# Dealing the copies of K and V anew over GpSimd, VectorE and ScalarE in a tree-masked attention kernel

## The chip, the cores and the metric

The kernel runs on one core of a Trainium2 chip. The metric is the device time of one execution in microseconds (us). The engines of the core are called by the profile's names: PE (TensorE: matmul, with PEld for its weight loads), DVE (VectorE), ACT (ScalarE), POOL (GpSimd), SP (SyncE). Loads and stores are DMA transfers; here nearly all of them are issued by GpSimd.

## The reference

Attention over 8 x 12 = 96 heads, 512 positions, 64 channels, with a mask that lets each position see itself and its ancestors in a binary tree (the parent of i is (i - 1) // 2):

```python
scale = 1.0 / np.sqrt(dim)
mask = np.zeros((seq, seq))
for i in range(seq):
    mask[i, i] = 1
    parent = i
    while parent > 0:
        parent = (parent - 1) // 2
        mask[i, parent] = 1
scores = np.einsum('bhqd,bhkd->bhqk', Q, K) * scale
scores = scores + (1 - mask) * (-1e9)
weights = np.exp(scores - np.max(scores, axis=-1, keepdims=True))
weights = weights / (np.sum(weights, axis=-1, keepdims=True) + 1e-10)
return np.einsum('bhqk,bhkd->bhqd', weights, V).astype(np.float32)
```

Q, K, V and the result are fp32 in HBM, 12.58 MB each.

## The kernel before

**Tiling.** The 96 heads are taken as 48 pairs i = 0 to 47; four pairs (8 heads) are a group g = i // 4, and 16 heads (two groups) are one block o of V. Because a node sees only its ancestors, most of the 512 x 512 scores are never computed: the nodes are reordered into units of 32, and each pair needs one full score tile (`scores1`, lines 494 and 499, exponentials at line 510) and a second, sparser one (`scores2`, lines 519 and 525, exponentials at line 541). The mask comes from small code matrices that are multiplied in (lines 494 and 519).

**The steps of a pair.** `transpose(i)` turns K and Q of a group on PE into the PSUM tile `kqp`, of which there is one (lines 375 and 397; four calls for a group: the first two turn K, the last two Q); `evac(i)` copies it to the SBUF tile `kq` on VectorE (line 444 after the first and the second call, line 436, one large copy, after the fourth). `scores1` and `scores2` multiply into the PSUM tiles `s1` and `s2`, one of each, and ScalarE takes the exponentials. `values(i)` multiplies with V into the PSUM tile `ob`, of which there is one (line 552), and `norm(i)` divides on VectorE (reciprocal at line 585, multiplication at line 590) into the output tile. `store(g)` sends a finished group of 8 heads, 1 MB, from GpSimd (line 598); the last four pairs are sent singly (line 607).

**Copies.** Two kinds of copy lie beside this. `lay_beside` (line 324) lays the two halves of K or of Q of one group side by side in `Kbeside` or `Qbeside` (two buffers each) before they can be transposed; it is needed for groups 3 to 11. `spread` (line 306) copies one of ten parts of a V block, for eight heads, from the loaded tile `vst` to the operand tile `vt` (two blocks): parts 0 to 3 are 32 x 512 words, parts 4 and 5 are 64 x 512, parts 6 to 9 are 32 x 256. All ten parts of eight heads must be there before `values` of the first pair that uses them.

**Order.** All order is written by hand. The engines run their lists in order and wait on semaphores. A start-up string (`EARLY`) holds the first steps; then turn i, for i from 6, runs the tokens "S T V": S is `scores1` and `scores2` of pair i, T is the next `transpose` with its `evac`, V is `values` and `norm` of pair i - 1. In the turns, T runs four pairs ahead of S; `TURNS` may change a turn's tokens: a second T in turn 17 puts T five pairs ahead from there on. L in a turn is a `lay_beside` of K on VectorE. After a turn's tokens come the V copies that `BY_VECTOR` and `BY_SCALAR` give to VectorE and ScalarE in that turn; from block 3 on, `STEADY_VECTOR` and `STEADY_SCALAR` deal parts 0, 1 and 3 to VectorE and part 2 to ScalarE in a fixed rhythm.

**GpSimd's list.** The string `POOL` is GpSimd's whole program: kN, qN, vN load eight heads from head N on (K and Q at line 267, V at line 257; three buffers of K, of Q and of V blocks), KN and QN are `lay_beside` of a group, c and t are V copies (t: parts 6 to 9, and from block 1 on also 4 and 5), x and e prepare the codes and the transposing matrices, sN stores a group, pN a single pair. A load needs a free buffer, so a load of K or Q of group g comes behind the copy of group g - 3.

Of the kernel before, what the change touches and what calls it, by code (L numbers as in the profile page):

```python
# [121 lines left out]
def kernel(  # L122
# [7 lines left out]
    nc = tc.nc  # L130
    B, H, S, D = Q.shape
# [87 lines left out]
    NV = 2  # L219
# [62 lines left out]
    def load_v(h0, n):  # L282
        return load(vsts, vloads, "vst", VB, Vr, h0, n)

    def spread(copy, o, part, h0, h1):

        vt, vst = vts[o % NV][:, :, :, :], vsts[o][:, :, :, :]
# [18 lines left out]
        return copy(out=dst, in_=src)  # L306
# [3 lines left out]
    def lay_beside(copy, name, g):  # L310

        kept = (ksts if name == "K" else qsts)[g]
        to = besides[name, g] = beside.tile([P, GP, 4, 2, D], bf16, name=f"{name}beside")
# [10 lines left out]
        copy(out=dst, in_=src)  # L324
# [218 lines left out]
    def values(i):  # L543

        if i < NP - 1:
            obs[i] = ob = psO.tile([P, 2, 512], fp32, name="ob")
        else:
            obs[i] = ob = psS.tile([P, 2, 512], fp32, name="s1")
        e1, e2, vt = ets[i], e2s[i % NE], vts[(2 * i // VB) % NV]

        def product(e, a, t, tile_v, lo=0, hi=128, **flags):
            nc.tensor.matmul(  # L552
                out=ob[lo:hi, a, 65 * t:65 * t + 65],
                lhsT=e[:, a, PLACE[t], lo:hi],
                rhs=vt[:, head(i, a) % VB, tile_v, 0:D + 1],
                **flags,
            )

        def halves(a):
            for t in (0, 1):  # L560
                product(e2, a, t, 1 + SELF[t], 0, 64, start=False, stop=t == 1)
                product(e2, a, t, 1 + t, 64, 128, start=False, stop=t == 1)

        for a in range(2):
            for t in range(4):
                product(e1, a, t, 0, start=t == 0, stop=False)
            for t in (2, 3):
                product(e2, a, t, 1 + t, start=False, stop=False)
            if i == NP - 1:
# [34 lines left out]
    def store_pair(eng, i, a=0, n=2):  # L604
# [12 lines left out]
    )  # L617

    def pool_program():

        ops = []
        for word in POOL.split():
# [6 lines left out]
            elif kind == "c":  # L629
                o, part, h0, h1 = n  # L630
                ops.append((spread, nc.gpsimd.tensor_copy, o, part, h0, h1))
            elif kind == "t":
                o, h0 = n
                ops += [
                    (spread, nc.gpsimd.tensor_copy, o, part, h0, h0 + KB)
                    for part in (6, 7, 8, 9) + ((), (4, 5))[min(o, 1)]
                ]
            elif kind == "s":
                ops.append((store, nc.gpsimd, n[0]))
# [8 lines left out]
    def ready(op, i):  # L648
# [18 lines left out]
    BY_VECTOR = {  # L667
# [11 lines left out]
    }  # L679
    BY_SCALAR = {  # L680
        0: [(0, 5, 0, 8)],
        4: [(0, 1, 8, 16), (0, 2, 8, 16)],
        7: [(1, 3, 0, 8)],
        8: [(1, 2, 0, 8)],
        11: [(1, 3, 8, 16)],
        12: [(1, 2, 8, 16)],
        13: [(2, 3, 0, 8)],
        15: [(2, 1, 0, 8)],
        17: [(2, 3, 8, 16)],
        18: [(2, 1, 8, 16)],  # L690
    }

    STEADY_VECTOR = {0: 0, 1: 1, 3: 3}
    STEADY_SCALAR = {2: 2}

    def spread_by(copy, table, steady, i):

        todo = list(table.get(i, []))
        for lead, h0 in ((4, 0), (0, 8)):
            o, j = divmod(i + lead, 8)  # L700
            if o >= 3 and o < NH // VB and j in steady:
                todo.append((o, steady[j], h0, h0 + 8))
        for args in todo:
            spread(copy, *args)

    program = pool_program()

# [16 lines left out]
        kept[0] = loads.tile([P, KB, 4, D], bf16, name=name)  # L724
        nc.vector.tensor_copy(out=kept[0][:, 0:2, :, :], in_=first[src][:, :, :, :])
    EARLY = "X K S Q D0 S A0 X6 T X D1 S X T V S T V T V T T A4 S D3 T V S T V"
    TURNS = {11: 'S T L4 V', 17: 'S T V T'}
    done, scored, valued = 1, 0, 0
    pool(-1)
    transpose(0)  # L730
    evac(0)

    def step(token):

        nonlocal done, scored, valued
        kind, n = token[0], token[1:]
# [15 lines left out]
        if kind == "X":  # L752
            spin("s1" if valued else "ob", int(n or 2))
        if kind == "D":
            for args in BY_VECTOR.get(int(n), []):
                spread(nc.vector.tensor_copy, *args)
        if kind == "A":
            for args in BY_SCALAR.get(int(n), []):
# [8 lines left out]
    for i in range(scored, NP + 1):  # L767
        turn = "S T V" if i not in TURNS else TURNS[i]
        for token in turn.split():
            step(token)  # L770
        spread_by(nc.vector.tensor_copy, BY_VECTOR, STEADY_VECTOR, i)
        spread_by(nc.scalar.copy, BY_SCALAR, STEADY_SCALAR, i)
        pool(valued)
        if i == NP - 1:
            store_pair(nc.sync, NP - 2)
# [33 lines left out]
```

## Time and profile before

| | us |
|---|---|
| Median of three runs (lowest to highest) | 133.6 (132.94 to 135.47) |
| The profiled execution, its own time | 132.84 |
| Its span in the profile, first to last instruction | 130.8 |

The span and the execution's own time differ by 2.0 us that lie around the profiled instructions. In the span PE is busy 88%, ACT 76%, POOL 74% and DVE 73%; the granted clock is 0.986. No engine is busy throughout, so the page has to be read by stages and by the chain of waits, and the transfers by their own rows: `DMA share` in a table of stretches is the time that packets took, summed over the 16 DMA engines and divided by 16 times the stretch (packets overlap, so it can be over 1), and GB/s counts what was written: a load reads 4 bytes of HBM for each 2 that it writes, since it converts fp32 to bf16 on the way. "To landing" is the time from the issue of a transfer to its completion.

### The profile page before, as it was taken

What the parts mean: (1) busy time and instruction counts of PE and PEld (TensorE: products, weight loads), DVE (VectorE), ACT (ScalarE), POOL (GpSimd) and SP (SyncE); (2) the same over time, 40 slices, a digit from 0 to 9 for tenths busy, and PEclk for the clock granted to TensorE, in tenths of its full rate; (3) what the DMA queues carried; (4) which work ended last, traced back from release to release, by engine and by line L of the source; (5) the groups of instructions that cost most, each with busy time, mean ns of one, the idle gap of its engine ahead of it and who ended that gap; (6) DMA issues with size and microseconds to landing.
All of it is one profiled execution on the core that took longest, in us unless ns stands there. A gap on an engine that the chain in (4) does not pass through costs nothing.

```text
span 130.8 us, 4949 instructions
## 1 busy us (share of the span) xinstructions
PE 115.4 (88%) x2132; PEld 82.6 (63%) x2133; DVE 95.9 (73%) x179; ACT 99.0 (76%) x160; POOL 96.3 (74%) x149
## 2 busy tenths in 40 slices
PE   4989996999998998995999997989989999989930
PEld 1444565776866676774776875767767777856620
DVE  4236778758958959774989798798998898775460
ACT  4339553787988988886778886887897897899920
POOL 6979978239899999999999999999996930202300
PEclk9999999999999999999999999999999999999995
DMA  4999999999999999999999999999999999999992
GB/s 124 195 185 205 209 185 211 201 211 205 210 197 217 201 206 202 209 205 207 212 199 211 202 209 207 205 210 232 336 220 357 406 401 401 401 402 401 384 352 94
DMA packets 24533, 32.13 MB, mean 246 GB/s; under 512 B 944, under 2 KB 15920, under 8 KB 24512
## 3 DMA queue, kind: packets, MB, share of 16 engines
q0 software_dynamic: 23232, 30.67, 110.9%
q1 hardware_dynamic: 720, 0.70, 1.7%
q10 hardware_dynamic: 560, 0.46, 1.0%
q8 instruction: 16, 0.26, 0.7%
q14 instruction: 5, 0.04, 0.1%
HBM read 37.86 MB, written 12.58 MB: 385 GB/s over the span
## 4 chain that ended last, share of the span: by engine, by line
PE 59%; DVE 25%; POOL 6%; issue 3%; ACT 3%; ACTq 0%; POOLq 0%
PE ob L552 16%; DVE kq L436 7%; PE s L494 7%; DVE of L590 7%; PE kqp L375 7%; PE s L499 6%; PE kqp L397 6%; PE s L519 5%; DVE vt L306 5%; PE s L525 5%; PE s L718 3%; POOL vt L306 3%; PE ob L718 2%; PE kqp L350 2%; DVE rec L585 2%
## 5 line engine op out<-in xcount | busy, mean ns | idle before, releaser
L510 ACT ACTIVATE e<-s 128x1024 bf16<-128x1024 f32 x48 | 49.1, 1023 | 21.3 <-PE s L499 20.9
L306 POOL COPY vt<-vst 32x256 uint32<-32x256 uint32 (+2 forms) x70 | 34.9, 499 | 8.9 <-DMA vst<-in_V_dram 5.7
L541 ACT ACTIVATE e<-s 128x384 bf16<-128x384 f32 (+1 forms) x92 | 41.4, 505 | 0.0
L552 PE MATMUL ob<-vt,e 128*128 128x65 bf16 (+1 forms) x940 | 36.9, 197 | 2.4 <-DVE of L590 2.1
L552 PEld LDWEIGHTS <-e 128*128 128x128 bf16 (+1 forms) x960 | 31.2, 102 | 7.9 <-DVE of L590 3.7
L590 DVE TENSOR_TENSOR of<-ob,rec 128x512 f32<-128x512 f32 x44 | 30.4, 691 | 1.5
L306 DVE COPY vt<-vst 32x512 uint32<-32x512 uint32 (+1 forms) x33 | 20.6, 625 | 1.0
L499 PE MATMUL s<-kq 64*128 64x512 bf16 x96 | 18.4, 379 | 2.1 <-DVE kq L436 2.1
L525 PEld LDWEIGHTS <-kq 64*128 64x128 bf16 x384 | 16.3, 110 | 6.3
L598 POOL DMA_DIRECT2D out_dram<-of x11 | 9.8, 897 | 13.5 <-DVE of L590 13.5
L585 DVE RECIPROCAL rec<-ob 128x8 f32<-128x8 f32 x47 | 9.6, 204 | 12.8 <-PE ob L552 12.5
L444 DVE COPY kq<-kqp 128x1024 bf16<-128x1024 bf16 x22 | 15.1, 687 | 4.9 <-PE kqp L375 4.4
L525 PE MATMUL s<-kq 64*128 64x160 bf16 (+1 forms) x384 | 17.9, 210 | 0.0
L494 PE MATMUL s<-qcoarse,codes 40*128 40x512 bf16 x88 | 17.2, 387 | 0.0
L519 PE MATMUL s<-qcoarse,codes 40*128 40x480 bf16 x88 | 16.3, 364 | 0.3
L436 DVE COPY kq<-kqp 128x2048 bf16<-128x2048 bf16 x11 | 13.5, 1224 | 2.2 <-PE kqp L397 1.8
L375 PE MATMUL kqp<-mixed,Kbeside 128*128 128x128 bf16 x144 | 11.1, 220 | 2.8 <-POOL Kbeside L324 1.7
L519 PEld LDWEIGHTS <-codes 40*128 40x128 bf16 x96 | 7.6, 95 | 8.4 <-issue 2.0
L306 ACT COPY vt<-vst 32x512 uint32<-32x512 uint32 (+1 forms) x17 | 10.7, 627 | 1.7 <-DMA vst<-in_V_dram 1.3
L397 PE MATMUL kqp<-ptile,Qbeside 128*128 128x128 bf16 x144 | 11.2, 220 | 0.2 <-DVE kq L444 0.2
L375 PEld LDWEIGHTS <-Kbeside 128*128 128x128 bf16 x144 | 8.3, 98 | 4.2 <-POOL Kbeside L324 2.0
L257 POOL DMA_DIRECT2D vst<-in_V_dram x12 | 10.9, 910 | 0.0
(45 smaller groups left out, 102.2 us busy)
## 6 DMA issues: line engine op xcount, KB each, us to landing
out_dram<-of POOLq DMA_DIRECT2D x11, 1024.0 KB, 15.6
vst<-in_V_dram POOLq DMA_DIRECT2D x12, 512.0 KB, 14.0
kst<-in_K_dram POOLq DMA_DIRECT2D x11, 512.0 KB, 11.9
qst<-in_Q_dram POOLq DMA_DIRECT2D x11, 512.0 KB, 12.3
out_dram<-ol POOLq DMA_DIRECT2D x2, 256.0 KB, 5.3
qst<-in_Q_dram POOLq DMA_DIRECT2D x3, 128.0 KB, 7.1
ol<-in_K_dram SPq DMA_DIRECT2D x1, 256.0 KB, 2.9
ol<-in_Q_dram ACTq DMA_DIRECT2D x1, 256.0 KB, 3.2
```

Of the source, the lines that this page charges most:

```text
L306: return copy(out=dst, in_=src)
L375: nc.tensor.transpose(out=dst, in_=src, identity=perm)
L397: nc.tensor.transpose(out=dst, in_=src, identity=eye[:, 0:128])
L436: return nc.vector.tensor_copy(out=dst, in_=src) if x == 3 else None
L494: nc.tensor.matmul(out=columns(g, sp[:, a, :], 0, 512), lhsT=k1code[64 * a:64 * a + CODE_ROWS, :], rhs=query_codes(i, a, 0, 0, 512), start ...
L499: nc.tensor.matmul(out=columns(g, sp[:, a, :], 0, 512), lhsT=keys(i, a, TOP), rhs=queries(i, a, 0, 512), start=False, stop=True,)
L510: nc.scalar.activation(out=dst, in_=src, func=AF.Exp, scale=scale)
L519: nc.tensor.matmul(out=columns(g, flat[:, a, :], 32, 512), lhsT=k2code[64 * a:64 * a + CODE_ROWS, :], rhs=query_codes(i, a, 1, 32, 512), s ...
L525: nc.tensor.matmul(out=columns(g, flat[:, a, :], lo, hi), lhsT=keys(i, a, TILE2[t]), rhs=queries(i, a, lo, hi), start=False, stop=t == 1,)
L541: nc.scalar.activation(out=dst, in_=src, func=AF.Exp, scale=scale)
L552: nc.tensor.matmul(out=ob[lo:hi, a, 65 * t:65 * t + 65], lhsT=e[:, a, PLACE[t], lo:hi], rhs=vt[:, head(i, a) % VB, tile_v, 0:D + 1], **flags,)
L590: nc.vector.tensor_tensor(out=dst, in0=o4[:, a:a + n, :, 0:D], in1=rec[:, a:a + n, :, :].to_broadcast([P, n, 4, D]), op=ALU.mult,)
```

## The change

GpSimd's list `POOL` is another one. It has the same loads and stores, the same copies of Q and the same V copies (parts 4 to 9 from block 1 on; the letter t is split into u for parts 6 to 9 and w for parts 4 and 5). Its order differs: among others v8 and the code preparation come earlier, the load k80 comes before k72, stores s0 and s1 come before the loads v88, k88 and q88, and s2 before q88. Of the K copies it keeps groups 6, 8 and 9; VectorE takes groups 3, 5, 7, 10 and 11 beside group 4, through L tokens in `TURNS`.

The V copies outside GpSimd are 50 as before, but VectorE has 26 instead of 33 and ScalarE 24 instead of 17, and all of them stand in the two tables: the steady rhythm is gone. The tokens D and A, which place a turn's VectorE and ScalarE copies, may now stand anywhere in a turn; without them they come last as before. The second T moves from turn 17 to turn 19.

```diff
     POOL = (
-        "k2.2 q2.2 v0 k4.4 q4.2 q6.2 k8 q8 e v8 c0.6.0.8 c0.7.0.8 c0.8.0.8 c0.9.0.8 x0 x64 k16 q16 v16 k24 q24 v24 "
-        "k32 t0.8 c0.3.8.16 c0.0.8.16 t1.0 K3 v32 q32 Q3 k40 t1.8 v40 q40 v48 t2.0 "
-        "Q4 k48 q48 v56 K5 t2.8 Q5 k56 q56 v64 t3.0 K6 k64 q64 v72 Q6 t3.8 "
-        "k72 q72 K7 Q7 v80 k80 q80 t4.0 K8 v88 s0 Q8 k88 q88 t4.8 s1 K9 Q9 t5.0 s2 K10 s3 Q10 t5.8 s4 K11 Q11 s5 s6 s7 s8 s9 s10 p44 p45 "
+        "k2.2 q2.2 v0 k4.4 q4.2 x0 q6.2 k8 v8 c0.7.0.8 x64 c0.9.0.8 c0.8.0.8 q8 c0.6.0.8 k16 q16 e v16 c0.3.8.16 "
+        "c0.0.8.16 k24 q24 v24 u0.8 k32 v32 u1.0 q32 k40 Q3 v40 w1.0 q40 u1.8 v48 w1.8 w2.0 q48 Q4 k48 u2.0 v56 "
+        "u2.8 w2.8 Q5 k56 q56 k64 Q6 w3.0 K6 q64 u3.0 v64 v72 u3.8 k80 q72 Q7 Q8 k72 q80 w4.0 K8 v80 w3.8 s0 s1 "
+        "K9 Q9 v88 w4.8 u4.0 u4.8 k88 s2 q88 w5.0 Q10 s3 w5.8 s4 s5 Q11 u5.0 s6 u5.8 s7 s8 s9 s10 p44 p45 "
     )
...
     BY_VECTOR = {
         0: [(0, 0, 0, 8), (0, 2, 0, 8), (0, 3, 0, 8)],
         1: [(0, 1, 0, 8), (0, 4, 0, 8)],
-        3: [(0, 4, 8, 16), (0, 5, 8, 16)],
-        7: [(1, 1, 0, 8)],
-        8: [(1, 0, 0, 8)],
-        11: [(1, 1, 8, 16)],
-        12: [(1, 0, 8, 16)],
-        14: [(2, 2, 0, 8)],
-        15: [(2, 0, 0, 8)],
-        17: [(2, 2, 8, 16)],
-        19: [(2, 0, 8, 16)],
+        3: [(0, 4, 8, 16), (0, 5, 8, 16), (0, 2, 8, 16), (0, 1, 8, 16)],
+        6: [(1, 0, 0, 8)],
+        7: [(1, 3, 0, 8)],
+        12: [(2, 2, 0, 8)],
+        13: [(1, 1, 8, 16)],
+        14: [(2, 0, 0, 8)],
+        16: [(2, 0, 8, 16)],
+        17: [(3, 0, 0, 8)],
+        22: [(3, 3, 0, 8)],
+        23: [(3, 3, 8, 16)],
+        24: [(3, 2, 8, 16)],
+        27: [(4, 0, 0, 8)],
+        29: [(4, 0, 8, 16), (4, 1, 8, 16)],
+        33: [(5, 2, 0, 8)],
+        37: [(5, 0, 8, 16)],
+        43: [(5, 3, 8, 16), (5, 2, 8, 16)],
     }
     BY_SCALAR = {
         0: [(0, 5, 0, 8)],
-        4: [(0, 1, 8, 16), (0, 2, 8, 16)],
-        7: [(1, 3, 0, 8)],
-        8: [(1, 2, 0, 8)],
-        11: [(1, 3, 8, 16)],
-        12: [(1, 2, 8, 16)],
-        13: [(2, 3, 0, 8)],
-        15: [(2, 1, 0, 8)],
-        17: [(2, 3, 8, 16)],
-        18: [(2, 1, 8, 16)],
+        7: [(1, 1, 0, 8), (1, 2, 0, 8)],
+        10: [(1, 0, 8, 16), (1, 2, 8, 16)],
+        12: [(1, 3, 8, 16)],
+        14: [(2, 1, 0, 8)],
+        15: [(2, 3, 8, 16)],
+        16: [(2, 3, 0, 8)],
+        17: [(3, 2, 0, 8)],
+        18: [(2, 1, 8, 16), (2, 2, 8, 16)],
+        19: [(3, 1, 0, 8)],
+        23: [(3, 1, 8, 16)],
+        25: [(3, 0, 8, 16)],
+        26: [(4, 2, 0, 8)],
+        29: [(4, 3, 0, 8)],
+        31: [(4, 1, 0, 8), (4, 2, 8, 16)],
+        33: [(5, 0, 0, 8)],
+        36: [(4, 3, 8, 16)],
+        39: [(5, 1, 0, 8)],
+        40: [(5, 3, 0, 8)],
+        41: [(5, 1, 8, 16)],
     }
-    STEADY_VECTOR = {0: 0, 1: 1, 3: 3}
-    STEADY_SCALAR = {2: 2}
...
-    TURNS = {11: 'S T L4 V', 17: 'S T V T'}
+    TURNS = {7: "S T L3 V", 10: "S T L4 V", 12: "S D T V", 13: "S D T V", 14: "S T A L5 V", 17: "S T D V", 19: "S T V T", 21: "S T V L7", 29: "S T D V", 31: "S T A V", 33: "S D T L10 V", 37: "S T D V", 38: "S L11 T V", 40: "S A T V"}
...
     for i in range(scored, NP + 1):
         turn = "S T V" if i not in TURNS else TURNS[i]
         for token in turn.split():
-            step(token)
-        spread_by(nc.vector.tensor_copy, BY_VECTOR, STEADY_VECTOR, i)
-        spread_by(nc.scalar.copy, BY_SCALAR, STEADY_SCALAR, i)
+            step(token, i)
+        if "D" not in turn:
+            step("D", i)
+        if "A" not in turn:
+            step("A", i)
         pool(valued)
```

An entry (o, part, h0, h1) is one V copy: block, part, first and last head of the block. The rest of the diff adds assertions that run while the program is built and hands the turn's number to `step`.

More of the change, by code (lines that the diff above doesn't have):

```diff
@@ L283, in load_v @@
         return load(vsts, vloads, "vst", VB, Vr, h0, n)
+    spreads = set()
+    done = scored = valued = 0
     def spread(copy, o, part, h0, h1):
+        assert 2 * valued >= VB * (o + 1 - NV)
+        spreads.update((o, part, h) for h in range(h0, h1))
         vt, vst = vts[o % NV][:, :, :, :], vsts[o][:, :, :, :]
@@ L312, in lay_beside @@
         kept = (ksts if name == "K" else qsts)[g]
+        assert done >= GP * (g - 1)
         to = besides[name, g] = beside.tile([P, GP, 4, 2, D], bf16, name=f"{name}beside")
@@ L548, in values @@
             obs[i] = ob = psS.tile([P, 2, 512], fp32, name="s1")
+        assert all((2 * i // VB, part, head(i, a) % VB) in spreads for part in range(10) for a in range(2))
         e1, e2, vt = ets[i], e2s[i % NE], vts[(2 * i // VB) % NV]
@@ L631, in pool_program @@
                 ops.append((spread, nc.gpsimd.tensor_copy, o, part, h0, h1))
-            elif kind == "t":
+            elif kind in "uw":
                 o, h0 = n
@@ L635, in pool_program @@
                     (spread, nc.gpsimd.tensor_copy, o, part, h0, h0 + KB)
-                    for part in (6, 7, 8, 9) + ((), (4, 5))[min(o, 1)]
+                    for part in {"u": (6, 7, 8, 9), "w": (4, 5)}[kind]
                 ]
@@ L681 @@
         0: [(0, 5, 0, 8)],
-        4: [(0, 1, 8, 16), (0, 2, 8, 16)],
-        7: [(1, 3, 0, 8)],
-        8: [(1, 2, 0, 8)],
-        11: [(1, 3, 8, 16)],
-        12: [(1, 2, 8, 16)],
-        13: [(2, 3, 0, 8)],
-        15: [(2, 1, 0, 8)],
-        17: [(2, 3, 8, 16)],
-        18: [(2, 1, 8, 16)],
-    }
-    STEADY_VECTOR = {0: 0, 1: 1, 3: 3}
-    STEADY_SCALAR = {2: 2}
[L696 to L704, printed above, removed]
+        7: [(1, 1, 0, 8), (1, 2, 0, 8)],
[17 more added lines that the diff above has]
+        41: [(5, 1, 8, 16)],
+    }
     program = pool_program()
@@ L731, with step @@
     evac(0)
-    def step(token):
+    def step(token, i=0):
         nonlocal done, scored, valued
@@ L754, in step @@
         if kind == "D":
-            for args in BY_VECTOR.get(int(n), []):
+            for args in BY_VECTOR.get(int(n or i), []):
                 spread(nc.vector.tensor_copy, *args)
         if kind == "A":
-            for args in BY_SCALAR.get(int(n), []):
+            for args in BY_SCALAR.get(int(n or i), []):
                 spread(nc.scalar.copy, *args)
```

## The prediction

> **What bounds the kernel now.** I read the page's engine shares and the rates of its slices first, then a table of stretches, then the issues of single transfers, and the waits last.
>
> ```profile
> span 130.8 us, 4949 instructions
> PE 115.4 (88%) x2132; PEld 82.6 (63%) x2133; DVE 95.9 (73%) x179; ACT 99.0 (76%) x160; POOL 96.3 (74%) x149
> DMA  4999999999999999999999999999999999999992
> ...
> HBM read 37.86 MB, written 12.58 MB: 385 GB/s over the span
> ```
>
> PE looks like the bound at 88%. But the row of the DMA engines is at 9 in every slice but the first and the last, and that is the one resource without a gap. The stretches say whether it is saturated or only occupied (busy time of PE, PEld, DVE, ACT and POOL, each with its instructions, then clock, DMA share, GB/s):
>
> ```profile
> 24.00:28.00 4.00, 4.00 (x91) 3.05 (x88) 3.13 (x6) 3.09 (x7) 0.00 (x0) 1.00 1.34 201
> 28.00:60.00 32.00, 29.71 (x572) 22.29 (x570) 24.21 (x45) 28.66 (x48) 29.80 (x48) 1.00 1.25 206
> 100.00:120.00 20.00, 19.24 (x374) 14.23 (x370) 15.96 (x31) 17.87 (x30) 5.50 (x7) 1.00 1.03 402
> ```
>
> From 24 to 28 us GpSimd issues nothing at all (x0), and the loads go on at 201 GB/s, as between 28 and 60 us where it issues all the time. In the stores the rate is 402. So the transfers stand in a queue, and their pace does not depend on when they are issued. How long that queue is:
>
> ```profile
> 19.69 0.70 POOL L267 DMA_DIRECT2D kst<-in_K_dram  x1 [0.92 <-PE kqp L375]
> kst<-in_K_dram POOLq DMA_DIRECT2D x1, 512.0 KB, 19.0
> ...
> 32.15 0.89 POOL L257 DMA_DIRECT2D vst<-in_V_dram  x1
> DMA to landing us min/median/max: 9.2/9.2/9.2
> ```
>
> The load k40, issued at 19.69, lands 19.0 us later, at 38.7. The next transfer of the list is issued at 32.15, 6.5 us before that, and lands at 41.35, 2.65 after its forerunner, which is 0.52 MB at 198 GB/s. Even after the longest pause of the issuer the queue had 6.5 us of work left. The tail:
>
> ```profile
> 125.59 1.08 SPq L607 DMA_DIRECT2D out_dram<-ol  x2
> 126.41 0.42 DVE L590 TENSOR_TENSOR ol<-s,rec 128x256 f32<-128x256 f32 x1
> 126.87 0.35 ACTq L607 DMA_DIRECT2D out_dram<-ol  x1
> ...
> out_dram<-ol SPq DMA_DIRECT2D x1, 256.0 KB, 3.7
> out_dram<-ol ACTq DMA_DIRECT2D x1, 128.0 KB, 3.1
> ```
>
> The last arithmetic ends at 126.83. The store of 256 KB issued at 125.59 lands at 129.3, the last 128 KB at 126.87 + 3.1 = 130.0. Between those lie two stores of 128 KB, 0.26 MB in 0.7 us, about 375 GB/s: the queue is full to its last byte. The sum of all transfers, by these rates: the loads write 18.9 MB (half of the 37.86 MB read) at 206 GB/s, 91.6 us; the stores 12.58 MB at 402 GB/s, 31.3 us; together 122.9 us of the 130. So the span is transfers end to end, with 0.9 us behind the last landing, and the chain of the engines is a second bound that fits into them. It has little to spare: the last store lands 3.1 us after its issue, and only the 0.7 us of the two stores ahead of it are surely queue.
>
> **Part 1, the transfers.** The same loads and stores are issued, so 122.9 us of queue remain. Two things can change: gaps, and the switches between loads and stores. Gaps: GpSimd loses five K copies and keeps all else, so on the whole it issues earlier; where it waits now is for landings (K9 behind its own load k72, Q11 behind q88), that is, for the queue itself, when the transfers issued before still stand in it (behind k72 come q80, v80, s0 and s1, 1.0 MB of loads and 2.1 MB of stores, 10 us). In the start q8 now stands behind v8 and seven small operations; I put its issue at about 13 us, when by my estimate all of v8 (2.5 us at 206 GB/s) and some 2 us of k8 are still to come. I take no gap. Switches:
>
> ```profile
> 77.37 0.90 POOL L257 DMA_DIRECT2D vst<-in_V_dram  x1
> 78.25 0.90 POOL L598 DMA_DIRECT2D out_dram<-of  x1
> ...
> out_dram<-of POOLq DMA_DIRECT2D x1, 1024.0 KB, 18.0
> vst<-in_V_dram POOLq DMA_DIRECT2D x1, 512.0 KB, 15.7
> ```
>
> Load v88 lands at 93.1, store s0 behind it at 96.25: 3.2 us for 1.05 MB that take 2.6 at 402 GB/s. A switch from loads to stores costs 0.6, of which I allow that the loads behind it win some back. Before there are two such switches (s0, s1), afterwards three (s0, s2, s3): +0.35, between 0 and 0.7.
>
> **Part 2, the copies.**
>
> ```profile
> L306 POOL COPY vt<-vst 64x512 uint32<-64x512 uint32 x20 | 12.6, 629 | 1.2
> L324 POOL COPY Kbeside<-kst 128x1024 uint32<-128x1024 uint32 x8 | 8.3, 1040 | 0.4
> L324 DVE COPY Kbeside<-kst 128x1024 uint32<-128x1024 uint32 x1 | 0.7, 682 | 0.0
> L306 DVE COPY vt<-vst 32x512 uint32<-32x512 uint32 (+1 forms) x33 | 20.6, 625 | 1.0
> L306 ACT COPY vt<-vst 32x512 uint32<-32x512 uint32 (+1 forms) x17 | 10.7, 627 | 1.7 <-DMA vst<-in_V_dram 1.3
> ```
>
> GpSimd: five K copies less, 5 x 1.04 = 5.2 us. VectorE: five K copies more, 5 x 0.68 = 3.4, seven V copies less, 7 x 0.625 = 4.4: 1.0 less. ScalarE: 7 x 0.627 = 4.4 more. What a copy costs in its place is another matter. On VectorE it depends on GpSimd:
>
> ```profile
> 93.81 1.05 POOL L324 COPY Qbeside<-qst 128x1024 uint32<-128x1024 uint32 x1
> ...
> 93.11 2.02 DVE L306 COPY vt<-vst 32x512 uint32<-32x512 uint32 x1
> ```
>
> This VectorE copy lasts 2.02 us and ends where GpSimd's copy of Q has ended; the mean is 0.625. So a K copy of 0.68 on VectorE may last up to 0.68 + 1.05. I take 0.68 + 0.2. The Trainium skill (SBUF — State Buffer, "Who interferes with whom") says that a VectorE copy in a two-port mode and a GpSimd instruction exclude each other for a whole instruction; the trace agrees (2.02 against 0.625), and the rule speaks against putting K copies on VectorE: by it all five could cost 5 x 1.73 = 8.7 us of VectorE instead of 3.4.
>
> **Part 3, PE's chain.**
>
> ```profile
> 34.07 0.39 PE L494 MATMUL s<-qcoarse,codes 40*128 40x512 bf16 x2
> 101.57 0.39 PE L494 MATMUL s<-qcoarse,codes 40*128 40x512 bf16 x2
> 102.98 0.78 PE L552 MATMUL ob<-vt,e 128*128 128x65 bf16 x20
> 103.69 0.39 PE L494 MATMUL s<-qcoarse,codes 40*128 40x512 bf16 x2
> ...
> 60.77 0.62 PE L375 MATMUL kqp<-mixed,Kbeside 128*128 128x128 bf16 x8 [1.50 <-POOL Kbeside L324]
> 33.73 1.06 POOL L324 COPY Qbeside<-qst 128x1024 uint32<-128x1024 uint32 x1
> 42.03 1.02 ACT L510 ACTIVATE e<-s 128x1024 bf16<-128x1024 f32 x1 [0.24 <-PE s L499]
> 44.50 1.02 ACT L510 ACTIVATE e<-s 128x1024 bf16<-128x1024 f32 x1
> ...
> PE ob L552 <- DVE of L590: 2.1, 7, 0.6
> PE kqp L375 <- DVE kq L436: 1.0, 2, 0.5
> ACT e L510 <- PE s L499: 20.9, 36, 2.9
> ```
>
> A turn begins with line 494. An undisturbed one is 2.12 us on PE (101.57 to 103.69), with V 1.4 us into it (102.98). A turn of ScalarE with one V copy in it is 2.47 (42.03 to 44.50), so each such copy costs up to 0.35 where nothing else waits.
> Gains: the copy K6 was 1.5 us late at 60.77; that goes, as GpSimd's shorter list reaches it early. PE's waits for VectorE, 2.1 at line 552 and 1.0 at line 375, have seven V copies less ahead of them: 2.0 of the 3.1 taken.
> Losses: in turn 9, V needs parts 4 and 5 of block 1 (w1.0). The new list has Q3, the load v40 and two copies of 0.63 there, and Q3 waits for its load as before; from its old start that is 33.73 + 1.06 + 0.89 + 1.26 = 36.9, or 0.5 earlier if the load alone holds it. V's old place is 34.07 + 1.4 = 35.5: +1.0. In turn 19 the second T needs the single `kqp`, whose large copy on VectorE (line 436, 1.2 us) starts only when the first T is done; V beside it hides some: +0.9. ScalarE's seven more copies: 7 x 0.35 = 2.5 at most, 1.3 taken, since some lie in turns that wait anyway.
> Sum: -1.5 - 2.0 + 1.0 + 0.9 + 1.3 = -0.3, between -4.6 (all gains, no loss) and +4.4 (1.0 + 0.9 + 2.5, no gain). What the chain gains is hidden by the queue of stores ahead of the last one; what it loses is hidden for 0.7 us. I take 0.
>
> **The sum.** On the profiled execution's own 132.84: 0 for gaps, +0.35 for switches, 0 for the chain: 133.2. The median of the runs shown is 133.6, 0.76 above the profiled one, which is the fastest of the four; the same shift would give 133.95. I forecast 133.6.
>
> **Rivals.** *The chain of waits is the bound.* PE is the busiest engine, and the waits named above are real; then the best case of part 3 counts in full, 132.84 - 4.6 = 128.2. Against it: no gap in the queue, 201 GB/s while nobody issues, and a last store that lands at the queue's pace. 122.9 us of transfers, some 2 us before the first and 0.9 behind the last leave 125.8 + 2.0 = 127.8 even if every switch and the start were free, so it is not wholly excluded. By the Trainium skill (DMA: Bandwidth & Descriptors, "Where 436 GB/s comes from") 435 GB/s is the ceiling; no stretch here shows it, the stores' 402 being nearest. *ScalarE becomes the bound*, on the other side. With its seven added copies at their whole 0.627, or 4.4 us, the last arithmetic ends at 126.8 + 4.4 = 131.2, and with 3.1 to the last landing, 0.9 behind it (130.8 less 129.97) and 2.0 around the span (132.84 less 130.8) the time is 137.2. It decides once the chain is 0.7 us late, and shows as over 2% some 3 us later. For it: turns 14 to 19 have seven copies in six turns, where ScalarE would need 6 x 1.84 + 7 x 0.63 = 15.4 us against 12.7 of PE (1.84 is 2.47 less a copy of 0.63). Against: in the whole run it stands idle behind PE for 20.9 us. *The queue runs dry*: GpSimd, held at K9 or Q11, issues v88 or s6 too late. The lead after the longest pause was 6.5 us, and I find some 4 at the worst place of the new list (q8); a pause of 2 us beyond it gives 135.2.
>
> **How the numbers follow.** Transfers bound, 133.6: 0.63, with a range of its own of 132.3 to 135. ScalarE or the copies as the bound, 137.2: 0.24. A dry queue, 135.2: 0.06. The chain of waits, 128.2: 0.07. A measurement of this kernel can tell about 2% from no change, that is 130.9 to 136.3. Faster than that comes from the chain alone, 0.07; slower from ScalarE and a few of the dry queues, 0.27; within, 0.66. For 8 in 10 the range goes from 132.2, which leaves out the chain, up to 137.4, which takes in most of ScalarE's case.
>
> **What would show it.** Right: the DMA row at 9 throughout, 402 GB/s in the stores, the last landing near 130.3, whatever turn 20 and the end of the arithmetic do. Switches: s2 landing over 3 us after k88. Turn 9: PE waits at line 552 for GpSimd's copy. Turn 19: line 375 waits for line 436. ScalarE: line 510 no longer waits for 20.9 us, and PE waits at line 519 or 494 for ScalarE. Wrong: a slice before the last with a DMA digit under 9, or arithmetic that ends past 128, with stores landing as soon as issued.

## The result, and the profile after

| | before | after |
|---|---|---|
| Median of 15 runs each (lowest to highest) | 133.95 (132.92 to 136.91) | 135.03 (134.16 to 136.4) |
| Time over before, 95% interval | 1 | 1.0102 (1.0062 to 1.0143) |
| The profiled execution, its own time | 132.84 | 135.99 |
| Its span | 130.8 | 133.6 |

The changed kernel is about 1.1 us, 1.0%, slower. That is within the 2% that the prediction called no change and inside its range of 132.2 to 137.4, but its interval does not reach 1: there is a loss to explain, and the prediction had none. The ratios, here and below, leave out executions that took over 1.5% longer than the fastest of their kernel; the medians hold all. The profiled execution of after took 135.99, 0.96 more than the median, so not all of the 2.8 us between the two spans belongs to the change.

The page of the changed kernel: span, engine shares, then the digits and rates of 40 slices.

```profile
span 133.6 us, 4952 instructions
PE 116.0 (87%) x2133; PEld 82.7 (62%) x2133; DVE 91.3 (68%) x177; ACT 102.9 (77%) x167; POOL 91.1 (68%) x144
DMA  3999999999999999999999999999999999999980
GB/s 127 179 172 204 198 205 210 193 212 204 209 200 212 203 208 202 211 204 208 214 208 199 204 215 208 210 275 396 228 152 324 309 392 405 391 396 389 397 312 32
HBM read 37.86 MB, written 12.58 MB: 377 GB/s over the span
```

The DMA digits stand at 9 as before, to the end of slice 38. The rates do not agree with them: slice 30 shows 152 GB/s, below anything that loads alone reach here (193 and up, once the start is over). A slice is 3.34 us, so this one runs from 97 to 100 us. As a table of stretches (busy time of PE, PEld, DVE, ACT and POOL, each with its instructions, then clock, DMA share, GB/s), first of the changed kernel:

```profile
28.00:60.00 32.00, 30.39 (x581) 22.55 (x578) 25.19 (x48) 29.21 (x50) 25.43 (x42) 1.00 1.25 206
95.00:100.00 5.00, 4.96 (x98) 3.66 (x95) 4.17 (x7) 3.95 (x8) 4.83 (x7) 1.00 1.22 168
99.00:100.00 1.00, 1.00 (x18) 0.61 (x17) 0.89 (x2) 0.46 (x2) 1.00 (x2) 1.00 1.16 96
100.00:120.00 20.00, 19.05 (x359) 13.77 (x361) 14.10 (x28) 18.60 (x32) 10.60 (x18) 1.00 1.03 366
```

and of the kernel before:

```profile
95.00:100.00 5.00, 4.34 (x84) 3.13 (x80) 4.54 (x10) 4.07 (x7) 4.68 (x8) 1.00 1.10 259
```

From 28 to 60 us both kernels move 206 GB/s. From 95 to 100 us the old one moves 259, the new one 168, and in the last of these microseconds 96, while the DMA share says 1.16. (The two kernels have different transfers in that stretch; e1 below has the same ones.) The share is the time that packets took, and packets that are in flight are counted whether data flow at half the rate or not.

What GpSimd did just before, in time order (start, duration, instruction), in the changed kernel:

```profile
86.27 1.04 POOL L330 COPY Kbeside<-kst 128x1024 uint32<-128x1024 uint32 x1 [3.63 <-DMA kst<-in_K_dram]
87.25 1.04 POOL L330 COPY Qbeside<-qst 128x1024 uint32<-128x1024 uint32 x1
88.23 0.88 POOL L257 DMA_DIRECT2D vst<-in_V_dram  x1
89.16 5.33 POOL L311 COPY vt<-vst 64x512 uint32<-64x512 uint32 x10
94.44 0.71 POOL L267 DMA_DIRECT2D kst<-in_K_dram  x1
95.14 0.92 POOL L605 DMA_DIRECT2D out_dram<-of  x1
96.05 0.71 POOL L267 DMA_DIRECT2D qst<-in_Q_dram  x1
```

and how long these transfers took from issue to landing (the last column, us; v88, k88 and s2, each the only one of its kind in the stretch):

```profile
out_dram<-of POOLq DMA_DIRECT2D x1, 1024.0 KB, 10.8
vst<-in_V_dram POOLq DMA_DIRECT2D x1, 512.0 KB, 11.1
kst<-in_K_dram POOLq DMA_DIRECT2D x1, 512.0 KB, 8.8
```

GpSimd waits 3.63 us at K9, until the load k72 has landed; from there on it waits for nothing. Between the loads v88 and k88 stand the words w4.8 u4.0 u4.8, ten V copies, 5.33 us in which it issues nothing. v88 lands at 88.23 + 11.1 = 99.3, so at the issue of k88, at 94.44, the queue had 4.8 us of work left. k88 lands at 94.44 + 8.8 = 103.2, some 4.0 us behind v88 (before rounding), where an undisturbed load of 0.52 MB stands 2.5 behind its forerunner. Some 1.5 us are lost here, though the queue never was without work.

The end of the changed kernel, in time order and as issues (the first answer is a timeline, the second lists issues):

```profile
126.60 0.42 DVE L597 TENSOR_TENSOR ol<-s,rec 128x256 f32<-128x256 f32 x1
127.05 0.35 ACTq L614 DMA_DIRECT2D out_dram<-ol  x1
```

```profile
out_dram<-ol SPq DMA_DIRECT2D x1, 128.0 KB, 6.1
out_dram<-ol ACTq DMA_DIRECT2D x1, 128.0 KB, 5.3
```

The last arithmetic ends at 127.02, 0.2 after that of before (126.83); but the store issued behind it takes 5.3 us to land where it took 3.1, so it lands at 127.05 + 5.3 = 132.4 instead of 130.0, with more of the queue still ahead of it. (In a second profile of the same kernel, below, this store takes 3.7.) So the engines arrive on time and the queue is late.

### The profile page after: what moved, and what is told of

It is laid out like the page before. It is cut to its first block, busy times and chain, and to the rows that moved or that the text cites. A ratio compares the mean times of both kernels' runs of the same rounds, so it can differ in the third digit from the quotient of the medians.

```text
span 133.6 us, 4952 instructions
## 1 busy us (share of the span) xinstructions
PE 116.0 (87%) x2133; PEld 82.7 (62%) x2133; DVE 91.3 (68%) x177; ACT 102.9 (77%) x167; POOL 91.1 (68%) x144
## 3 DMA queue, kind: packets, MB, share of 16 engines
HBM read 37.86 MB, written 12.58 MB: 377 GB/s over the span
## 4 chain that ended last, share of the span: by engine, by line
PE 52%; ACT 16%; DMA 12%; DVE 7%; issue 4%; POOL 3%; ACTq 0%; POOLq 0%
PE ob L559 14%; ACT e L547 7%; PE s L500 7%; PE kqp L381 7%; PE kqp L403 7%; PE s L525 7%; DMA vst<-in_V_dram 6%; ACT e L516 6%; DMA qst<-in_Q_dram 5%; PE s L531 5%; PE s L505 5%; DVE kq L442 5%; ACT vt L311 3%; POOL qcoarse L245 1%; DVE of L597 1%
## 5 line engine op out<-in xcount | busy, mean ns | idle before, releaser
L516 ACT ACTIVATE e<-s 128x1024 bf16<-128x1024 f32 x48 | 49.2, 1024 | 18.6 <-PE s L505 17.8
L311 POOL COPY vt<-vst 32x256 uint32<-32x256 uint32 (+2 forms) x70 | 34.3, 489 | 10.1 <-DMA vst<-in_V_dram 7.2
L330 POOL COPY Qbeside<-qst 128x1024 uint32<-128x1024 uint32 x9 | 9.8, 1084 | 12.6 <-DMA qst<-in_Q_dram 8.5
L311 ACT COPY vt<-vst 32x512 uint32<-32x512 uint32 (+1 forms) x24 | 15.0, 625 | 0.5
L525 PEld LDWEIGHTS <-codes 40*128 40x128 bf16 x96 | 7.6, 95 | 11.2 <-issue 6.1
L311 DVE COPY vt<-vst 32x512 uint32<-32x512 uint32 (+1 forms) x26 | 12.4, 476 | 2.5 <-DMA vst<-in_V_dram 1.9
L381 PE MATMUL kqp<-mixed,Kbeside 128*128 128x128 bf16 x144 | 11.1, 220 | 0.7 <-DVE kq L442 0.7
L403 PE MATMUL kqp<-ptile,Qbeside 128*128 128x128 bf16 x144 | 11.2, 220 | 0.0
```

The lines of the kernel that those rows point to most:

```text
L381: nc.tensor.transpose(out=dst, in_=src, identity=perm)
L403: nc.tensor.transpose(out=dst, in_=src, identity=eye[:, 0:128])
L516: nc.scalar.activation(out=dst, in_=src, func=AF.Exp, scale=scale)
L525: nc.tensor.matmul(out=columns(g, flat[:, a, :], 32, 512), lhsT=k2code[64 * a:64 * a + CODE_ROWS, :], rhs=query_codes(i, a, 1, 32, 512), s ...
```

## The experiments

A word first for all of them: "lead" is the time for which the queue still had work when a transfer was issued, that is, the landing of the transfer ahead of it less its issue. Ratios are to the kernel before, run on the same chip, with 95% intervals.

**The late feed undone (e1).** Load k88 goes ahead of the ten copies, nothing else changes.

```diff
-            "K9 Q9 v88 w4.8 u4.0 u4.8 k88 s2 q88 w5.0 Q10 s3 w5.8 s4 s5 Q11 u5.0 s6 u5.8 s7 s8 s9 s10 p44 p45 "
+            "K9 Q9 v88 k88 w4.8 u4.0 u4.8 s2 q88 w5.0 Q10 s3 w5.8 s4 s5 Q11 u5.0 s6 u5.8 s7 s8 s9 s10 p44 p45 "
```

> The changed kernel with one word of GpSimd's list moved: the load k88 comes right behind v88, ahead of ten V copies (w4.8 u4.0 u4.8, 5.3 us) that stood between them. In the changed kernel k88 was issued at 94.4, 4.8 us before the transfer ahead of it landed, and landed 4.0 us behind that one instead of 2.5. Late feed (k88 reaches the queue too late, 1.5 us lost): the step of k88's landing is 2.5 again, the time falls by 1.0 to 1.5 us against the changed kernel, a ratio of 0.998 to 1.003 to the kernel before. The start (the loss lies before 14 us) or ScalarE's copies: nothing changes, 1.007 to 1.014. Chance hits on the queue that fall as they fall in every kernel: nothing changes either, 1.007 to 1.014.

Measured: 132.67, ratio 1.0028 (0.9999 to 1.0056), span 130.4. The same stretches and the issue rows in e1:

```profile
95.00:100.00 5.00, 4.95 (x99) 3.74 (x96) 4.02 (x7) 4.06 (x7) 4.79 (x7) 1.00 1.21 262
99.00:100.00 1.00, 1.00 (x19) 0.68 (x16) 0.82 (x2) 0.48 (x1) 0.96 (x2) 1.00 1.08 371
```

```profile
vst<-in_V_dram POOLq DMA_DIRECT2D x1, 512.0 KB, 10.7
kst<-in_K_dram POOLq DMA_DIRECT2D x1, 512.0 KB, 12.4
```

The rate is back at 262, and GpSimd is as busy as in after (4.79 of 5 us against 4.83): what it does is the same, only when it issues differs. With v88 issued at 87.72 and k88 at 88.59, they land at 98.4 and 101.0, 2.5 apart before rounding. Nearly all of the loss is gone.

**Loads first (e2).** The three switches from loads to stores (s0, s2, s3) become one: v88, k88 and q88 go ahead of s0.

```diff
-            "u2.8 w2.8 Q5 k56 q56 k64 Q6 w3.0 K6 q64 u3.0 v64 v72 u3.8 k80 q72 Q7 Q8 k72 q80 w4.0 K8 v80 w3.8 s0 s1 "
-            "K9 Q9 v88 w4.8 u4.0 u4.8 k88 s2 q88 w5.0 Q10 s3 w5.8 s4 s5 Q11 u5.0 s6 u5.8 s7 s8 s9 s10 p44 p45 "
+            "u2.8 w2.8 Q5 k56 q56 k64 Q6 w3.0 K6 q64 u3.0 v64 v72 u3.8 k80 q72 Q7 Q8 k72 q80 w4.0 K8 v80 v88 k88 q88 w3.8 s0 s1 "
+            "K9 Q9 w4.8 u4.0 u4.8 s2 w5.0 Q10 s3 w5.8 s4 s5 Q11 u5.0 s6 u5.8 s7 s8 s9 s10 p44 p45 "
```

> The changed kernel with the last three loads, v88, k88 and q88, issued right behind v80 and so ahead of every store. Late feed: as with k88 moved alone, 0.998 to 1.003. Switches between loads and stores (my forecast allowed 0.35 us for one more of them; here is one instead of three): up to 0.7 us faster still, 0.993 to 0.998. The start or ScalarE's copies: 1.007 to 1.014.

Measured: 132.83, ratio 1.0027 (1.0003 to 1.0051). Three switches (e1) and one (e2) give the same time: the price of a switch, which the prediction put at 0.35 for one more of them, is not to be found.

**The old start (e3).** Only the words of the list up to v16 are those of before.

```diff
-            "k2.2 q2.2 v0 k4.4 q4.2 x0 q6.2 k8 v8 c0.7.0.8 x64 c0.9.0.8 c0.8.0.8 q8 c0.6.0.8 k16 q16 e v16 c0.3.8.16 "
+            "k2.2 q2.2 v0 k4.4 q4.2 q6.2 k8 q8 e v8 c0.6.0.8 c0.7.0.8 c0.8.0.8 c0.9.0.8 x0 x64 k16 q16 v16 c0.3.8.16 "
```

> The changed kernel with GpSimd's list of the kernel before from the first word to v16 (q8 ahead of v8, the code preparation behind the first V copies); all later words are the changed kernel's. The start: v0 lands near 9.6 instead of 11.2 and the time falls by 1.0 to 1.6 us, ratio 0.998 to 1.003. Late feed, or ScalarE's copies: 1.007 to 1.014 as for the changed kernel, and k88's landing still comes 3.5 to 4 us behind that of the transfer before it.

Measured: 133.96, ratio 1.0071 (1.0035 to 1.0106). A loss stays, and so does the late feed: k88 lands 4.6 us behind v88. The interval reaches those of after, so whether the start has a share of its own is not settled by this run. Its profiled execution took 135.32, 1.4 more than the median, but its trace shows a step of the prediction that after hides. PE's instructions at line 559 and the start of the next turn (line 500) in e3:

```profile
36.24 0.28 PE L559 MATMUL ob<-vt,e 128*128 128x65 bf16 x4
37.67 0.65 PE L559 MATMUL ob<-vt,e 128*128 128x65 bf16 x16 [1.15 <-POOL vt L311]
38.25 0.39 PE L500 MATMUL s<-qcoarse,codes 40*128 40x512 bf16 x2
```

In the turn from 34.80 to 38.25 PE waits 1.15 us for GpSimd's copies w1.0.

**The chain shortened (e4).** The kernel before without the code matmuls of lines 494 and 519, so that its scores are not masked.

```diff
-                out=columns(g, sp[:, a, :], 0, 512), lhsT=k1code[64 * a:64 * a + CODE_ROWS, :],
-                rhs=query_codes(i, a, 0, 0, 512), start=True, stop=False,
...
-                rhs=queries(i, a, 0, 512), start=False, stop=True,
+                rhs=queries(i, a, 0, 512), start=True, stop=True,
...
-                out=columns(g, flat[:, a, :], 32, 512), lhsT=k2code[64 * a:64 * a + CODE_ROWS, :],
-                rhs=query_codes(i, a, 1, 32, 512), start=True, stop=False,
...
-                    rhs=queries(i, a, lo, hi), start=False, stop=t == 1,
+                    rhs=queries(i, a, lo, hi), start=True, stop=True,
```

> The kernel before without the mask: the four matmuls of the codes (lines 494 and 519) are left out of each pair, so that the scores are not masked; the same transfers, copies, exponentials and norms. PE's turn falls from 2.12 to about 1.35 us, ScalarE's 1.8 us becomes the turn's length, and the chain of the engines is 5 to 12 us shorter. Transfers bound: the time stays within 1% of the kernel before, ratio 0.99 to 1.01, and the loads wait for nothing. Chain bound: 121 to 128 us, ratio 0.91 to 0.96.

Measured: 132.87, ratio 1.0014 (0.9992 to 1.0036). The expectation was too large in size: the last arithmetic ends only 1.7 us earlier, at 125.1, since PE now waits longer for others (in total 3.8 us for GpSimd's copies of K, 1.7 before; 4.3 for the large copy on VectorE, 2.1 before). The sense of it stands: 1.7 us off the chain buys no time at all, for the last stores then take 4.8 and 3.9 us to land instead of 3.3 and 3.1.

**The loss made in the old kernel (e5).** The kernel before, with k88, q88 and the stores s1 to s3 moved behind its copies.

```diff
-            "k72 q72 K7 Q7 v80 k80 q80 t4.0 K8 v88 s0 Q8 k88 q88 t4.8 s1 K9 Q9 t5.0 s2 K10 s3 Q10 t5.8 s4 K11 Q11 s5 s6 s7 s8 s9 s10 p44 p45 "
+            "k72 q72 K7 Q7 v80 k80 q80 t4.0 K8 v88 s0 Q8 t4.8 K9 Q9 t5.0 K10 Q10 k88 q88 s1 s2 s3 t5.8 s4 K11 Q11 s5 s6 s7 s8 s9 s10 p44 p45 "
```

> The kernel before with the late feed put into it: in GpSimd's list the loads k88 and q88 stand behind t4.8 K9 Q9 t5.0 K10 Q10 and ahead of s1, instead of right behind s0 and Q8. Nothing else changes; the chain of the engines needs K11 and Q11 only in turn 39 and later. By GpSimd's rows k88 is then issued near 91.5 instead of 80.1, some 5 us before s0 lands (before: 16 us). Late feed: a hole as in the changed kernel, k88 landing 3.5 to 4.5 us behind s0 instead of 2.3, ratio 1.005 to 1.012. If 5 us of lead are enough for the queue: 1.000 to 1.003, and the loss in the changed kernel is of another kind.

Measured: 134.14, ratio 1.0105 (1.0058 to 1.0153), as much as the changed kernel loses. The table of stretches of e5:

```profile
95.00:100.00 5.00, 4.96 (x100) 3.72 (x97) 4.56 (x9) 4.76 (x9) 4.68 (x9) 1.00 1.02 158
98.00:99.00 1.00, 1.00 (x20) 0.54 (x18) 0.83 (x3) 0.81 (x3) 0.94 (x3) 1.00 0.88 100
```

The lead at k88 was 4.2 us (s0 lands at 95.8, k88 is issued at 91.63), and the rate falls to 100 GB/s, as in after. One thing differs from what was expected: k88 itself lands only 2.3 us behind s0, and it is q88, issued right behind it with 5.8 us of queue still ahead, that stands 4.3 behind k88. The lost time need not show on the transfer that came late.

**The dose (e6, twice, and after again).** k88 in two other places of the changed kernel, and the changed kernel unaltered beside them. In the first, k88 stands between u4.0 and u4.8; in the second, w5.0 goes ahead of it too.

```diff
-            "K9 Q9 v88 w4.8 u4.0 u4.8 k88 s2 q88 w5.0 Q10 s3 w5.8 s4 s5 Q11 u5.0 s6 u5.8 s7 s8 s9 s10 p44 p45 "
+            "K9 Q9 v88 w4.8 u4.0 k88 u4.8 s2 q88 w5.0 Q10 s3 w5.8 s4 s5 Q11 u5.0 s6 u5.8 s7 s8 s9 s10 p44 p45 "
```

```diff
-            "K9 Q9 v88 w4.8 u4.0 u4.8 k88 s2 q88 w5.0 Q10 s3 w5.8 s4 s5 Q11 u5.0 s6 u5.8 s7 s8 s9 s10 p44 p45 "
+            "K9 Q9 v88 w4.8 u4.0 u4.8 w5.0 k88 s2 q88 Q10 s3 w5.8 s4 s5 Q11 u5.0 s6 u5.8 s7 s8 s9 s10 p44 p45 "
```

> The changed kernel with k88 four V copies earlier (ahead of u4.8, behind u4.0): issued some 1.7 us earlier, about 6.5 us before v88 lands instead of 4.8. Late feed with a threshold between 5 and 8 us: part of the hole is left, k88 lands 2.5 to 3.5 us behind v88, ratio 1.003 to 1.007. Another cause: as the changed kernel in this job.

> The changed kernel with k88 two V copies (w5.0, 1.3 us) later: about 3.5 us of lead instead of 4.8. Late feed: the hole grows by about what the lead loses, k88 lands 4.5 to 5.5 us behind v88, 1.0 to 1.3 us slower than the changed kernel, ratio 1.015 to 1.020. Another cause: as the changed kernel in this job.

> The changed kernel itself, on the chip of the three others, so that they are compared on one chip: ratio 1.006 to 1.014 by its first measurement, with k88 landing 3.5 to 4.5 us behind v88.

Measured, with e1 and the first comparison of after, ordered by lead (landing of v88 less issue of k88):

| kernel | lead at k88, us | k88 lands behind v88, us | time over before (95%) |
|---|---|---|---|
| e6, w5.0 ahead too | 3.7 | 4.0 | 1.016 (1.0112 to 1.0208) |
| after | 4.8 | 4.0 | 1.0102 (1.0062 to 1.0143) |
| after, again | 5.0 | 3.7 | 1.0121 (1.0059 to 1.0183) |
| e6, between the copies | 6.9 | 2.5 | 1.0003 (0.9971 to 1.0035) |
| e1, ahead of all copies | 9.9 | 2.5 | 1.0028 (0.9999 to 1.0056) |

The stretch from 95 to 100 us of the two ends of the dose, first with 3.7 us of lead, then with 6.9:

```profile
95.00:100.00 5.00, 4.95 (x99) 3.75 (x96) 4.01 (x7) 4.08 (x7) 4.87 (x7) 1.00 1.12 149
```

```profile
95.00:100.00 5.00, 4.96 (x92) 3.55 (x90) 4.14 (x8) 3.96 (x8) 4.75 (x7) 1.00 1.20 260
```

The same copies and stores on the same engines, 149 against 260 GB/s. For e6 between the copies part of the hole was expected; it had none. So the limit lies between 5.0 and 6.9 us of queued work at this place, and it is the place of one load that decides. The second profile of the changed kernel also tells what of its first profile belongs to the change: it has the same hole with a span of 131.2 and a time of 133.61, so the 133.6 of the first contains delays of that one execution. (In the run with 3.7 us k88 was expected 4.5 to 5.5 behind v88, and it lands no later than in after; s2 behind it comes late as well, 3.35 instead of 2.6, and that would be the rest of its larger loss.)

**Old start and early k88 together (e7).** The edits of e1 and e3 in one kernel.

> The changed kernel with both edits: k88 right behind v88, and GpSimd's list of the kernel before from the first word to v16. Late feed alone makes the change's loss: no different from k88 moved alone (ratio 1.0028, interval 0.9999 to 1.0056). A share of the start: 0.997 to 1.000, and v0's landing comes less than 3.5 us behind q2's.

Measured: 135.05, ratio 1.0106 (1.0027 to 1.0185): a miss. Its profiled execution (135.95, the longest of those timed) has no hole at k88; there the loads are late from the start. v0 lands at 11.3, 5.4 us behind q2 (in e1 at 9.6, 3.5 behind it), and v88 at 100.6 (in e1 at 98.4). An early turn of PE in order of time, in e7:

```profile
22.31 0.39 PE L500 MATMUL s<-qcoarse,codes 40*128 40x512 bf16 x2
25.68 0.64 PE L381 MATMUL kqp<-mixed,kst 128*64 128x128 bf16 x16 [1.17 <-DMA kst<-in_K_dram]
26.25 0.79 PE L559 MATMUL ob<-vt,e 128*128 128x65 bf16 x20
26.97 0.39 PE L500 MATMUL s<-qcoarse,codes 40*128 40x512 bf16 x2
```

From one start of a turn (line 500) to the next it takes 4.7 us, 1.17 of them a wait for the load k16; the last arithmetic ends at 129.1 instead of 126.8, and the time follows. The two profiles of the changed kernel have v0 at 11.2 and at 9.8, so a late v0 can come with an execution, whatever the list. Whether it does in the other executions of e7 no trace shows, so its loss stays open.

**w1.0 ahead of Q3 (e10).** e7 with one more step moved, against the wait for w1.0 that e3 showed.

```diff
-            "c0.0.8.16 k24 q24 v24 u0.8 k32 v32 u1.0 q32 k40 Q3 v40 w1.0 q40 u1.8 v48 w1.8 w2.0 q48 Q4 k48 u2.0 v56 "
+            "c0.0.8.16 k24 q24 v24 u0.8 k32 v32 u1.0 q32 k40 w1.0 Q3 v40 q40 u1.8 v48 w1.8 w2.0 q48 Q4 k48 u2.0 v56 "
```

> The version that the runs point to: the changed kernel with k88 right behind v88, GpSimd's start of the kernel before (q8 ahead of v8, so that the fourth transposition of group 1 doesn't wait for q8), and w1.0 ahead of Q3, so that V of turn 9 doesn't wait for parts 4 and 5. Chain: turn 9 takes 2.3 instead of 3.45 us, and the last arithmetic ends 0.5 to 1.0 us before that of the version with k88 moved alone (126.9), if the first loads come as early. The transfers stay as long as they are. Two bounds that lie together: 0.997 to 1.002. If the chain alone were the bound: 0.992 to 0.996.

Measured: 132.99, ratio 1.0036 (1.0009 to 1.0063). The wait for GpSimd is gone, the turn that took 3.45 us in e3 takes 2.8 (34.33 to 37.12) where 2.3 was expected, and the arithmetic ends at 126.5, 0.4 earlier than in e1. The time gains nothing by it. No version tried beats the kernel before.

**Less in the queue (e8).** The kernel before without store s5, 1 MB of the 12.58 (group 5's rows are not written).

```diff
-            "k72 q72 K7 Q7 v80 k80 q80 t4.0 K8 v88 s0 Q8 k88 q88 t4.8 s1 K9 Q9 t5.0 s2 K10 s3 Q10 t5.8 s4 K11 Q11 s5 s6 s7 s8 s9 s10 p44 p45 "
+            "k72 q72 K7 Q7 v80 k80 q80 t4.0 K8 v88 s0 Q8 k88 q88 t4.8 s1 K9 Q9 t5.0 s2 K10 s3 Q10 t5.8 s4 K11 Q11 s6 s7 s8 s9 s10 p44 p45 "
```

> The kernel before without the store of group 5 (1 MB, 2.6 us of the queue; its rows of the result are not written). Transfers bound to the last: the queue is 2.6 us shorter, and the time falls until the chain's own end shows. The last arithmetic ends at 126.9 as before, and an unhindered store of 128 KB behind it takes at least the 2.4 us that the first transfers took, so the time falls by 0.7 us at most, ratio 0.994 to 0.998: the two bounds lie that close. Transfers not the bound: 1.000. Transfers the only bound: 0.980.

Measured: 133.35, ratio 1.0001 (0.9966 to 1.0037), though 2.6 us of transfers are gone; of the 0.7 us that could be gained nothing shows. In e8 a stretch near the end, and the last stores:

```profile
120.00:122.00 2.00, 2.00 (x38) 1.32 (x39) 0.94 (x3) 1.83 (x4) 0.89 (x1) 1.00 0.28 107
```

```profile
out_dram<-ol SPq DMA_DIRECT2D x1, 128.0 KB, 1.7
out_dram<-ol ACTq DMA_DIRECT2D x1, 128.0 KB, 2.6
```

Now the queue does run empty, and here the DMA share shows it, 0.28. The stores land 1.7 and 2.6 us after their issue, but the last is issued behind the last arithmetic as ever, which here ends at 127.3, 0.4 later than before, so the last landing stays at 129.9. With e4 this brackets the kernel before: cutting only the chain or only the queue gives nothing, so the two end together.

**The second T back in turn 17 (e9).** e1 with the second T where it was; one execution, no interval. Of the line, the part that differs:

```diff
-    TURNS = {... 17: "S T D V", 19: "S T V T", ...}
+    TURNS = {... 17: "S T D V T", ...}
```

> The changed kernel with k88 right behind v88 and the second T back in turn 17. My term for turn 19 was +0.9 us on PE's chain: here turn 19 is near 2.1 to 2.5 us instead of 3.75, turn 17 near 3.3 instead of 2.7, and turn 20 begins 0.5 to 1.0 us earlier. The time stays that of k88 moved alone, as transfers bound it (one look: within 1%).

Measured: one execution of 134.2. What PE waits for in turn 19 now, and the start of turn 20, in e9:

```profile
61.24 0.62 PE L381 MATMUL kqp<-mixed,Kbeside 128*128 128x128 bf16 x8 [0.63 <-POOL Kbeside L330]
62.40 0.39 PE L500 MATMUL s<-qcoarse,codes 40*128 40x512 bf16 x2
```

Turn 20, the first behind both places, starts at 62.40 against 62.52 in e1. Turn 17 starts at 54.50 against 54.18, as this execution was behind already, so the turns from 17 to 19 take 0.4 us less, where 0.5 to 1.0 was expected: a wait of 0.63 for GpSimd has taken the place of one of 0.70 for VectorE.

## Why the prediction failed, point by point

**The bound: right, and half of it missing.** Transfers end to end set the time, and a late queue is nearly the whole of the loss (e1, e5, the dose). That the chain "fits into them" with little to spare was right too, but it makes two bounds rather than one (e4, e8); the 0.7 us itself no run shows, as a queue 2.6 us shorter gained nothing.

**Gaps in part 1: this is the step that failed.** "I take no gap." The prediction walked the new list for the places where GpSimd waits (K9 behind k72, Q11 behind q88, q8 in the start) and overlooked a place where it only works: the ten copies between v88 and k88, 5.3 us by after's row. The row of the larger of these copies, 0.63 each, stands in the prediction; the run of them was never summed. When k72 lands the prediction had 10 us of queue behind it. Less K9 and Q9 (2.1), the issue of v88 (0.9) and the ten copies (5.3), and with the 2.5 us that v88 adds, 4.2 are left at k88; 4.8 were measured. It also took a lead of some 4 us for safe. Here 4.8 us cost 1.5, and 6.9 cost nothing. At q8, the place that the prediction called the worst, the lead came out at 4.8 as well, and no time was lost there: q8, issued at 14.27, landed 2.5 us behind v8. One number of us, then, is no law; one difference between the two places is that stores stand in the queue ahead of k88, and whether that is the cause was not tried.

**The rival that was right.** "The queue runs dry" had the mechanism, with 0.06 and at the wrong transfers (v88 or s6 in place of k88). It priced the case at 135.2; the median is 135.03. That nearness is luck: the price was a pause of 2 us taken at will, and the hole is 1.5.

**The sign to look for: wrong meter.** "A slice before the last with a DMA digit under 9" is not to be seen at the hole. The digit stays 9 and the share above 1 while the rate is 96 to 168 GB/s. (The 8 of slice 39 is the end of the last stores, from 127 us on.) Read by GB/s, the page shows the hole at once.

**Switches: mis-sized.** +0.35 was taken, none is measured (1.0028 with three, 1.0027 with one). The late landing of s0 in before was taken for a price of the change of direction on the strength of one transfer. The sign named for it, s2 over 3 us behind k88, fails: s2 lands 2.7 behind it in after and in e1. What made s0 late in before was not tried.

**The chain of part 3: right in sum.** The first matmul of turn 20 and of turn 44, in before:

```profile
61.94 0.39 PE L494 MATMUL s<-qcoarse,codes 40*128 40x512 bf16 x2
...
116.95 0.39 PE L494 MATMUL s<-qcoarse,codes 40*128 40x512 bf16 x2
```

and in after, with the second T of turn 19 and the waits of ScalarE for the scores (in total, times, longest), from another view, below:

```profile
62.59 0.61 PE L381 MATMUL kqp<-mixed,Kbeside 128*128 128x128 bf16 x8 [0.70 <-DVE kq L442]
63.13 0.39 PE L500 MATMUL s<-qcoarse,codes 40*128 40x512 bf16 x2
...
117.13 0.39 PE L500 MATMUL s<-qcoarse,codes 40*128 40x512 bf16 x2
```

```profile
ACT e L516 <- PE s L505: 17.8, 23, 5.1
```

Turn 20 begins 1.2 us later than before, turn 44 only 0.2. This is the long execution, with v0 late; in the second profile of the same kernel turn 20 begins at 62.22, 0.3 later, and turn 44 at 116.66, 0.3 earlier, which is the -0.3 that was summed (0 was taken). That it fits so closely is luck in part: of the losses in the sum, the 1.0 of turn 9 did not come there (that turn takes 2.4 us). Turn 19 waits 0.70 for the large copy on VectorE, where 0.9 was taken. Turn 9 waits for w1.0 as described, 1.15 in e3 where 1.0 was taken; in after it does not, because the turn itself comes later, at 35.80 instead of 34.80 as in e3. Part of that is q8 behind v8, for which PE waits 0.55 us near 21 us; the prediction had looked at q8 for the queue alone. What the first twenty turns lose, the later ones win back.

**The copies of part 2.** GpSimd 96.3 to 91.1, 5.2 less as predicted; ScalarE 99.0 to 102.9, 3.9 more for 4.4; VectorE 95.9 to 91.3, 4.6 less where 1.0 was predicted. Two groups of after show it (busy time, mean ns of one), the first from the page, the second from the table that keeps shapes apart:

```profile
L311 DVE COPY vt<-vst 32x512 uint32<-32x512 uint32 (+1 forms) x26 | 12.4, 476 | 2.5 <-DMA vst<-in_V_dram 1.9
```

```profile
L330 DVE COPY Kbeside<-kst 128x1024 uint32<-128x1024 uint32 x6 | 4.4, 725 | 0.2
```

A V copy on VectorE now takes 0.476 in the mean for 0.625, a K copy 0.725, not the 0.88 that was taken. In before four V copies took 1.18 to 2.02 us, each beside a copy of K or Q on GpSimd, 3.9 us more than four at the new mean; in after none took over 0.76. The Trainium skill (SBUF — State Buffer, "Who interferes with whom") says that a VectorE copy in a two-port mode and a GpSimd instruction exclude each other. These four agree with it, and so does a K copy of 1.30 beside a copy of Q in the second profile of the changed kernel. But the six K copies of the row took 0.68 to 0.79, four of them beside instructions of GpSimd, so the 1.73 each that the prediction named as possible did not come.

**ScalarE as the bound.** It got its copies and still stood idle behind PE for 17.8 us, where it had been 20.9; it did not become the bound.

**What stays open.** e1 and e2 lie at 1.003 and the version of e6 between the copies at 1.0003, with intervals that overlap. The interval of e2, like that of e10 (1.0036), does not reach 1. Whether some 0.3% remains after the feed is mended is not settled.

## What to carry to other kernels

Where transfers stand in one queue from end to end, list every stretch in which the issuer issues nothing, work as well as waits, and compare it with the queue's lead at that place; here, ahead of k88, a lead of 5 us was too short and 7 was enough, while at q8 4.8 was enough. Look for holes in the rate and not in the busy share, and put the loads ahead of a run of copies. When neither a shorter chain nor a shorter queue gains anything, the two end together, and only a change that shortens both can pay.

## What was not expected of the hardware

The queue loses rate while it has work: in after it sinks from 235 GB/s (95 to 96 us) through 145, 172 and 192 to 96 (99 to 100 us), before v88 lands at 99.3, though k88 had been issued at 94.44. The core has 16 DMA engines. The Trainium skill (DMA: Bandwidth & Descriptors, "Why a DMA increments its semaphore by 16 and not by 1") says that these engines finish independently. The trace agrees: its file holds sixteen completions for each transfer, which no view prints one by one, and those of v88 lie between 96.1 and 99.3 us.

One would think that the engines that were done early found nothing behind v88, but the packets, which the file holds too, speak against it. Packets of 2 KB, the size of k88's, begin at 95.9, before the first of the sixteen completions of v88. From there to 101.4 us 56 of them take 0.2 to 1.6 us each, where an undisturbed one takes 0.17; in e1, and in e6 with k88 between the copies, none does. What they take beyond 0.17 is 19.3 us in all, 1.2 for each of 16 engines, most of the 1.5 by which k88 is late. So the time is lost inside the packets of the late load, and this is why the busy share stays high. Why these packets take so long no run here tells.

The price of a late feed seems to grow with the delay: none at 6.9 us of lead, 1.0 to 1.2% at 5.0 and 4.8, 1.6% at 3.7 (the last intervals overlap), and in every case the transfer ahead had not yet landed.
